# Seven products for the last pair of projections of the first unit, and three changes of order in the stages behind it

## Chip, cores and metric

The kernel runs on one core of a Trainium2 chip. The metric is the device time of one execution in microseconds (us), the median over several runs. The inputs and the outputs lie in the chip's memory; all of the arithmetic is float32, done on TensorE as pairs of fp32r parts (a rounded "hi" part and the remainder "lo").

## The reference

One layer of a streaming encoder, for 2048 frames of a new stream and 32 frames of a running one, width 1024:

```
hn   = rmsnorm(h, g_mix);  proj = hn @ w_in            # 1024 -> 3072
h_A, b_A, c_A, z_A, v_B, z_B = split(proj)             # six kinds of 512 columns
yA   = b_A * conv3(c_A * h_A) * silu(z_A)
yB   = (pooled(v_B) - v_B) @ pool_w * pool_scale * silu(z_B)
h    = h + concat(yA, yB) @ w_out
gate = sigmoid(rmsnorm(h, g_ple) @ w_ple_gate)
h    = h + (p @ w_ple) * gate                          # p: embedding frames, 256 wide
y    = rmsnorm(h, g_final)
```

The states of the convolution and of the pooling are returned too.

## The kernel before

**Stages.** (1) The input projection, from 0 to 532 us of the profile. (2) The first seven embedding products `p @ w_ple` (532 to 552 us). (3) The output projection with `w_out`, 16 tiles of 128 frames taken in pairs (552 to 717 us). (4) The other embedding products (717 to 747 us). (5) The gate with `w_ple_gate`, again in pairs of tiles, and the closing norm.

**Products.** A product of two fp32 operands is three matmuls per 128 rows of contraction: hi by hi, hi by lo, lo by hi (`FINE`). A weight or a frame is *put* into this form by a cast on ScalarE (hi) and a subtraction on VectorE (lo): `split`, L81 and L84, for frames and for the weights of stage 1, `weight_first` L203 and `weight_second` L210 for the weights of stages 3 and 5. In most places a two by two block product isn't done as eight half products but as seven (a Strassen-Winograd scheme): sums and differences of the blocks are put instead of the blocks, and three PSUM banks X, Y and Z gather the results. A half product is 12 matmuls of 128x512 (`half_product`, L646; in stages 3 and 5 `product`, L185).

**Stage 1.** The frames are taken in two groups of 1024 (two blocks of 512), and the 512 columns of each kind in four slices `j`. A `Unit` is one group and one slice. Its six kinds form the pairs zb and v, c and h, za and b. For all units but the first, `Unit.seven` runs the three pairs through `Unit.pair` (seven half products each; weights by `pair_weights`, whose sums and differences are L606 and L618 on VectorE). The first unit runs `Unit.plain`, since the normed, transposed frames and their sums are still being made: each kind is projected block by block (`project`, four half products for the two blocks, 48 matmuls), and a generator, `second_block`, makes the second block's frames and the differences T1 to T4 (L797) in twelve steps. `plain` calls `next(second)` where a step is to come in program order. T4 doesn't fit into the buffers at that time: its four quarters go to memory (`to_memory`, L546, the queue of GpSimd, POOL), and L1290 reads it back on SyncE's queue (SP) behind the unit, into a buffer (`seventh`) that the first unit's own frames (`B0_12`) hold until the last block-1 product has read them. The weights come through three raw buffers (`raw_weight`, L578) and six buffers of put weights (`wtile`).

**Who sets the order.** The program is written as a sequence of instructions, and the framework lists them for each engine before the run: by its own model of times it takes, among those that are ready, the one that stands first in the program. Each engine then runs its list strictly in order. `keep_in_program_order` (`pin`) ties an instruction behind the one written before it on its engine; `issue_after` ties the instructions of a block that are on one engine behind a given one. `bufs` of a pool says how many buffers of a tag there are; a new tile waits for the release of an old one.

**Stage 3, first pair of tiles (`o0`).** `seven(..., late=True)` runs X (frames A11 by weights 11), half of Z (S1 by T1), X (S2 by T2), the other half of Z, X (S3 by T3), then Y (A12 by 21), Z (S4 by 22) and X (A22 by T4). Carries of the banks X and Z are copies by ScalarE for this pair (L1320); the adds of the results are on VectorE (L1315). The functions in `LATER` are called between these products: `third` (weights T3), `left` (weights 21 and 22, then the frames' cast A12 by `more(0)`), `later(1)` (S4), `later("T4", 2)`. The differences for T2, T3 and T4 are L195; those of T3 are done by GpSimd before. The weight rows come in as `wo_t` (upper, `tops`) and `wo_b` (lower, `bots`).

**Stage 4.** L1501 loads the embedding's weights `wq` on SP, then the lower rows of the gate's weights (`wg_b`, L1386) are queued behind them with `issue_after(last_q.ins)`. The embedding frames `pps` (L129) come one tile of 128 frames after the other into the four buffers of the pool `st`, which the carries of stage 3 use too.

Of the kernel before, what the change touches and what calls it, by code (L numbers as in the profile page):

```python
# [36 lines left out]
def trunk(ctx, tc, x_p, x_s, c_conv, c_pool, p_p, p_s, g_mix, w_in, conv_w, conv_b, pool_w,  # L37
# [86 lines left out]
            wp.append(t)  # L124
        return wp

    def load_pps(t, i, queue):
        n = 4 * tiles[i][1]
        queue.dma_start(t.rearrange("p a k n -> p (a k n)")[:, :n].bitcast(F32), pp_d[i, :, :n])  # L129
        return t  # L130

    def short_embed_product(ps, pps, wp, cs, n):

# [51 lines left out]
                nc.tensor.matmul(ps[:n], lhs[:, k, a, :n], w[b][:, k], start=start and k + q == 0,  # L185
                                 stop=k == KH - 1 and q == 2, skip_group_check=True)

    def weight_source(W, q, k, top, bot, pin=False, sums=nc.vector):

        b11, b12 = top[:, :NH], top[:, NH:]  # L190
        b21, b22 = (bot[:, :NH], bot[:, NH:]) if bot is not None else (None, None)
        t, x, y = {"11": (b11, None, None), "T1": (b11, b12, b11), "T2": (b11, b22, b11), "T3": (b12, b22, b12),
                   "22": (b22, None, None), "21": (b21, None, None), "T4": (b21, b21, b11)}[q]
        if x is not None:
            ins = sums.tensor_tensor(t, x, y, op=ALU.subtract)  # L195
            if pin and sums is nc.vector:
                tc.keep_in_program_order(ins)
        return t

# [12 lines left out]
            tc.keep_in_program_order(ins)  # L212
        return ins

    def weight_parts(W, tops, bots, *names, order=range(KH), pin=False, sums=nc.vector):

        for q in names:
            at = lambda k: (W, q, k, tops[k], bots[k] if bots else None)
            todo = [(k, weight_source(*at(k), pin, sums)) for k in order[:2]]
            for k in order[2:]:  # L220
                weight_first(W, todo[0], q, pin)
                following = (k, weight_source(*at(k), pin, sums))
# [143 lines left out]
    def seventh(name):  # L366
        return w7.tile([P, 2 * KH * NH], F32R, tag="h", name=name)
# [31 lines left out]
    with ExitStack() as s1:  # L399
# [197 lines left out]
        def pair_weights(gi, ka, kb, j, name, ring, s_ring, ring_b, pin):  # L597

            s_t = (wk.tile([P, KH, P], F32, tag="s", name=f"s_{name}") if s_ring is None else
                   s_ring(f"s_{name}"))
            ra = raw_weight(ka, j, f"{name}a", ring)
            a11, a12 = ra[:, :KH], ra[:, KH:]
            sub = lambda o, x, y: nc.vector.tensor_tensor(o, x, y, op=ALU.subtract)  # L606
            if (ka, j) in kept:
                k1, k3 = kept.pop((ka, j))
                rb = ring_b(f"raw_{name}b")
                col = cols[kb] * WA + j * P  # L610
                nc.sync.dma_start(s_t, k1)
                nc.sync.dma_start(rb[:, :KH], k3)
                raw_loads.append(nc.sync.dma_start(rb[:, KH:], w_in[NH:, col:col + P].rearrange("(k p) n -> p k n", p=P)))
                s3, a22 = rb[:, :KH], rb[:, KH:]
            else:
                rb = raw_weight(kb, j, f"{name}b", ring_b)
                a21, a22 = rb[:, :KH], rb[:, KH:]
                total = nc.vector.tensor_tensor(s_t, a21, a22, op=ALU.add)  # L618
                if pin:
                    in_turn(total)  # L620
                sub(a21, a11, a21)
                s3 = a21
                if gi == 0:
# [212 lines left out]
        class Unit:  # L836
# [65 lines left out]
            def plain(self):  # L902
# [29 lines left out]
                for b in blocks:  # L932
                    ps = product_of("h", b, wh)
                    nc.vector.tensor_tensor(self.place(U, HU, b), ps, self.cols(c_s, b), op=ALU.mult)
                    self.conv(b)
                    if b:
                        next(second)
                wza = weights("za", j, f"za{tag}")
                for b in blocks:
                    z = self.cols(V, b)  # L940
                    nc.scalar.activation(z, product_of("za", b, wza), AF.Silu)
                    c = self.cols(c_s, b)
                    nc.vector.tensor_tensor(c, c, z, op=ALU.mult)
                    if b:
                        next(second)
                wb = weights("b", j, f"b{tag}")
                for b in blocks:
                    ps = product_of("b", b, wb)
                    y = self.cols(c_s, b)
                    nc.vector.tensor_tensor(y, ps, y, op=ALU.mult)  # L950
                    self.store(j, b, c_s)


            def pair(self, ka, kb, B, D, done, ring, s_ring=None, pin=False):
# [39 lines left out]
            def seven(self, B, aside, both=False):  # L994
# [24 lines left out]
                        self.conv(1)  # L1019


                za = [self.cols(V, b) for b in range(2)]
                gb = self.cols(U, 0)

                def za_done(b):
                    nc.scalar.activation(za[b], za[b], AF.Silu)
                    mul(self.cols(c_s, b), self.cols(c_s, b), za[b])

                def b_second():
                    mul(self.cols(c_s, 1), self.cols(c_s, 1), gb)  # L1030
                    self.store(j, 1, c_s)

                def b_first(ps):
                    mul(self.cols(c_s, 0), ps, self.cols(c_s, 0))
                    self.store(j, 0, c_s)

                ring = [spare_ring if both and i == 1 else raw_ring for i in range(3)]
                pairs = [
                    ("zb", "v", B, {(0, 0): self.cols(zs, 0), (0, 1): self.cols(zs, 1), (1, 1): at(V, HV, 1)},
                     {(0, 0): lambda ps: zb_done(0), (0, 1): lambda ps: zb_done(1), (1, 1): nothing, (1, 0): v_first}),  # L1040
                    ("c", "h", B, {(0, 0): self.cols(c_s, 0), (0, 1): self.cols(c_s, 1), (1, 1): at(U, HU, 1)},
                     {(0, 0): nothing, (0, 1): h_second, (1, 1): nothing, (1, 0): h_first}),
                    ("za", "b", B, {(0, 0): za[0], (0, 1): za[1], (1, 1): gb},
                     {(0, 0): lambda ps: za_done(0), (0, 1): lambda ps: (za_done(1), b_second()), (1, 1): nothing,
                      (1, 0): b_first})]

                def first_mix():
                    self.mix(0)
# [233 lines left out]
        for gi, tbs in enumerate(GROUPS):  # L1282
            if gi == 1:
                B = load_group(1)
            for j in range(4):
                u = Unit(gi, tbs, j)
                if gi + j == 0:
                    u.plain()
                    B0["T4"] = piece_of(seventh("B0_T4"), 0)
                    nc.sync.dma_start(B0["T4"].bitcast(F32), p_d["T4"])  # L1290
                    p_d["T4"] = tc.dram_tile([P, KH, 2, NB], F32, name="p_dT4b")
                    aside = at_pace(next_columns(3, 0, 1, 2), 13, 18)
                    continue
# [6 lines left out]
    with ExitStack() as s2:  # L1300
# [152 lines left out]
        gate_rows = iter(range(KC))  # L1453
        waiting = []

# [42 lines left out]
        got = {0: load_pps(st.tile([P, 2, 2, P], F32R, tag="t", name=f"pps_{EARLY}"), EARLY, nc.sync)}  # L1498
        for k in range(2):
            for h in range(2):  # L1500
                last_q = nc.sync.dma_start(wp[k][h].bitcast(F32), wl_d[k][h])  # L1501
# [327 lines left out]
```

## Time and profile before

| | |
|---|---|
| median of 3 runs | 930.83 us (930.36 to 932.89) |
| the profiled execution | 930.23 us |
| its span, first to last instruction | 928.4 us |
| TensorE (PE) busy | 902.4 us |
| VectorE (DVE) busy | 699.7 us |
| ScalarE (ACT) busy | 458.8 us |
| mean granted TensorE clock | 0.995 |

All starts below are us from the start of the span. A row of a timeline has the start, the duration, the engine, the line, the operation, out<-in, the count, and in brackets the idle time of the engine ahead of it with what ended it. Rows of several merged instructions have the duration from the first start to the last end. A row of a list of stretches has, for each engine, the busy time and the count, then the granted clock, the DMA engines' busy share and GB/s. A row of the DMA issues ends with the size and the us from issue to landing.

### The profile page before, as it was taken

What the parts mean: (1) busy time and instruction counts of PE and PEld (TensorE: products, weight loads), DVE (VectorE), ACT (ScalarE), POOL (GpSimd) and SP (SyncE); (2) the same over time, 40 slices, a digit from 0 to 9 for tenths busy, and PEclk for the clock granted to TensorE, in tenths of its full rate; (3) what the DMA queues carried; (4) which work ended last, traced back from release to release, by engine and by line L of the source; (5) the groups of instructions that cost most, each with busy time, mean ns of one, the idle gap of its engine ahead of it and who ended that gap; (6) DMA issues with size and microseconds to landing.
All of it is one profiled execution on the core that took longest, in us unless ns stands there. A gap on an engine that the chain in (4) does not pass through costs nothing. (4 is left out here: it accounts for less than half of the span.)

```text
span 928.4 us, 12196 instructions
## 1 busy us (share of the span) xinstructions
PE 902.4 (97%) x4186; PEld 724.1 (78%) x4186; DVE 699.7 (75%) x1144; ACT 458.8 (49%) x828; POOL 164.5 (18%) x313
## 2 busy tenths in 40 slices
PE   8999999999999999999999998999999899999996
PEld 6788887878788888766688876878888788778885
DVE  6895789797993688746668689765645988888884
ACT  7752555465453354523444366434434865555543
POOL 2200121222121123100010051111111211121212
PEclk9999999999999999999999999999999999999998
DMA  8164396747599776777743685886767776576653
GB/s 271 53 206 168 105 263 188 221 153 247 165 335 427 177 220 182 244 216 238 235 141 135 218 304 188 256 252 218 232 210 281 279 270 192 164 228 203 215 186 110
DMA packets 113243, 199.56 MB, mean 215 GB/s; under 512 B 13206, under 2 KB 69950, under 8 KB 112157
## 3 DMA queue, kind: packets, MB, share of 16 engines
q1 hardware_dynamic: 88733, 117.19, 40.5%
q0 software_dynamic: 22000, 77.21, 24.6%
q10 hardware_dynamic: 2448, 4.39, 1.3%
q8 instruction: 33, 0.54, 0.2%
q14 instruction: 29, 0.24, 0.1%
HBM read 133.06 MB, written 65.67 MB: 214 GB/s over the span
## 5 line engine op out<-in xcount | busy, mean ns | idle before, releaser
L185 PE MATMUL x_o<-wo_T,y_S 128*128 128x512 f32 x192 | 46.3, 390 | 1.3 <-ACT c_o L1320 1.3
L185 PE MATMUL z_o<-wo,y_S 128*128 128x512 f32 x192 | 47.6, 390 | 0.0
L185 PE MATMUL z_g<-wg,g_S 128*128 128x512 f32 x192 | 47.3, 392 | 0.0
L185 PE MATMUL x_o<-wo,y 128*128 128x512 f32 x192 | 45.5, 390 | 0.9 <-DVE x L1315 0.9
L185 PEld LDWEIGHTS x_o<-wo_T,y_S 128*128 128x128 f32 x192 | 35.9, 188 | 9.3 <-ACT c_o L1320 1.9
L185 PEld LDWEIGHTS x_o<-wo,y 128*128 128x128 f32 x192 | 36.0, 188 | 8.9 <-DVE x L1315 1.3
L185 PEld LDWEIGHTS z_o<-wo,y_S 128*128 128x128 f32 x192 | 36.0, 188 | 7.7 <-DVE y_S L84 0.3
L646 PE MATMUL z_ch<-B,w_ch_S 128*128 128x512 f32 x168 | 40.8, 392 | 1.1 <-ACT U L966 1.1
L646 PE MATMUL x_zab<-B,w_zab_S 128*128 128x512 f32 x168 | 41.1, 392 | 0.8 <-ACT V L966 0.6
L646 PE MATMUL x_ch<-B,w_ch_S 128*128 128x512 f32 x168 | 41.8, 392 | 0.0
L185 PEld LDWEIGHTS z_g<-wg,g_S 128*128 128x128 f32 x192 | 35.6, 188 | 7.4 <-ACT c_g L1553 0.2
L646 PE MATMUL z_zab<-B,w_zab_S 128*128 128x512 f32 x168 | 41.1, 392 | 0.0
L646 PE MATMUL x_zbv<-B,w_zbv_S 128*128 128x512 f32 x168 | 40.8, 391 | 0.0
L646 PE MATMUL z_zbv<-B,w_zbv_S 128*128 128x512 f32 x168 | 40.7, 391 | 0.0
L646 PEld LDWEIGHTS z_ch<-B,w_ch_S 128*128 128x128 f32 x168 | 31.3, 188 | 8.8 <-ACT U L966 1.5
L646 PEld LDWEIGHTS x_zab<-B,w_zab_S 128*128 128x128 f32 x168 | 31.2, 188 | 8.8 <-ACT V L966 1.0
L646 PEld LDWEIGHTS x_zbv<-B,w_zbv_S 128*128 128x128 f32 x168 | 31.3, 188 | 7.5 <-issue 0.8
L646 PEld LDWEIGHTS z_zab<-B,w_zab_S 128*128 128x128 f32 x168 | 31.2, 188 | 7.5 <-issue 0.8
L646 PEld LDWEIGHTS x_ch<-B,w_ch_S 128*128 128x128 f32 x168 | 31.3, 188 | 7.2 <-issue 0.8
L646 PEld LDWEIGHTS z_zbv<-B,w_zbv_S 128*128 128x128 f32 x168 | 31.3, 188 | 7.2 <-issue 0.8
L81 ACT CAST y_S<-y_fS 128x512 fp32r<-128x512 f32 x28 | 17.1, 619 | 26.5 <-PE x_o L185 12.1
L1572 DVE SCALAR_TENSOR_TENSOR h<-h,rstd_f,g_bc 128x1024 f32<-128x1024 f32 (+1 forms) x15 | 19.3, 1284 | 14.5 <-POOL rstd_f L77 12.9
(562 smaller groups left out, 2310.9 us busy)
## 6 DMA issues: line engine op xcount, KB each, us to landing
wn<-in_w_in_dram SPq DMA_DIRECT2D x24, 512.0 KB, 4.1
p_dT<-T POOLq DMA_DIRECT2D x16, 512.0 KB, 5.4
y<-y_d SPq DMA_DIRECT2D x16, 512.0 KB, 4.8
h<-h_d POOLq DMA_DIRECT2D x16, 512.0 KB, 4.8
e<-e_d SPq DMA_DIRECT2D x15, 512.0 KB, 4.6
x<-in_x_prompt_dram SPq DMA_DIRECT2D x14, 512.0 KB, 4.4
out_dram<-h POOLq DMA_DIRECT2D x14, 512.0 KB, 3.3
B<-p_d POOLq DMA_DIRECT2D x3, 2048.0 KB, 16.0
```

The costliest lines, as they stand in the source:

```text
L81: ins = nc.scalar.copy(hi, src)
L185: nc.tensor.matmul(ps[:n], lhs[:, k, a, :n], w[b][:, k], start=start and k + q == 0, stop=k == KH - 1 and q == 2, skip_group_check=True)
L646: nc.tensor.matmul(ps, lhs[:, k, x], b[:, k, y], start=start and k + q == 0, stop=stop and k == KH - 1 and q == 2, skip_group_check=True)
L1572: nc.vector.scalar_tensor_tensor(h[:n], h[:n], rf[:n], g_bc[:n], op0=ALU.mult, op1=ALU.mult)
```

## The change

Four edits:

1. The first unit's third pair (za, b) runs through `pair` with seven half products. `plain` calls `next(second)` in both rounds of `h` and no more behind them, T4 is read back ahead of the pair on POOL's queue, and the pair's dictionary moves into a method, `third`, that both `plain` and `seven` use. `pair_weights` doesn't keep the first unit's sums in memory.
2. In stage 4 the second embedding frames are loaded right behind `wq`, and the gate's lower rows are queued behind them.
3. T3's differences for `w_out` are done by VectorE, pinned.
4. In `LATER`, the cast of A12 comes ahead of the weights 21, and the weights 22 with S4 move to the next step.

```diff
-                if gi == 0:
+                if gi == 0 and j:
                     kept[ka, j] = k1, k3 = [tc.dram_tile(...)]
...
                     self.conv(b)
-                    if b:
-                        next(second)
-                wza = weights("za", j, f"za{tag}")
-                for b in blocks:
-                    z = self.cols(V, b)
-                    nc.scalar.activation(z, product_of("za", b, wza), AF.Silu)
-                    c = self.cols(c_s, b)
-                    nc.vector.tensor_tensor(c, c, z, op=ALU.mult)
-                    if b:
-                        next(second)
-                wb = weights("b", j, f"b{tag}")
-                for b in blocks:
-                    ps = product_of("b", b, wb)
-                    y = self.cols(c_s, b)
-                    nc.vector.tensor_tensor(y, ps, y, op=ALU.mult)
-                    self.store(j, b, c_s)
+                    next(second)
+                B0["T4"] = piece_of(seventh("B0_T4"), 0)
+                nc.gpsimd.dma_start(B0["T4"].bitcast(F32), p_d["T4"])
+                p_d["T4"] = tc.dram_tile([P, KH, 2, NB], F32, name="p_dT4b")
+                for _ in self.pair(*self.third(B0), raw_ring):
+                    pass
...
                 if gi + j == 0:
                     u.plain()
-                    B0["T4"] = piece_of(seventh("B0_T4"), 0)
-                    nc.sync.dma_start(B0["T4"].bitcast(F32), p_d["T4"])
-                    p_d["T4"] = tc.dram_tile([P, KH, 2, NB], F32, name="p_dT4b")
...
         def third():
-            hold.append(weight_parts(W, tops, bots, "T3", pin=True, sums=nc.gpsimd))
+            hold.append(weight_parts(W, tops, bots, "T3", pin=True))

         def left():
+            more(0)
             weight_parts(W, tops, bots, "21", pin=True)
+
+        def right():
             weight_slot(W, "wo", "22", "T4")
             hold.append(weight_parts(W, tops, bots, "22", pin=True))
-            more(0)
+            more(1)

-        LATER = {1: third, 2: left, 3: later(1), 4: later("T4", 2)}
+        LATER = {1: third, 2: left, 3: right, 4: later("T4", 2)}
...
         for k in range(2):
             for h in range(2):
-                last_q = nc.sync.dma_start(wp[k][h].bitcast(F32), wl_d[k][h])
-        with tc.issue_after(last_q.ins):
+                nc.sync.dma_start(wp[k][h].bitcast(F32), wl_d[k][h])
+        got[1] = st.tile([P, 2, 2, P], F32R, tag="t", name=f"pps_{EARLY + 1}")
+        second_pps = load_pps(got[1], EARLY + 1, nc.sync, True)
+        with tc.issue_after(second_pps.ins):
             bots = rows_of_weight(cmb, "wg_b", g_d, 1)[0]
```

More of the change, by code (lines that the diff above doesn't have):

```diff
@@ L125, in load_wp, with load_pps @@
         return wp
-    def load_pps(t, i, queue):
+    def load_pps(t, i, queue, ins=False):
         n = 4 * tiles[i][1]
-        queue.dma_start(t.rearrange("p a k n -> p (a k n)")[:, :n].bitcast(F32), pp_d[i, :, :n])
-        return t
+        load = queue.dma_start(t.rearrange("p a k n -> p (a k n)")[:, :n].bitcast(F32), pp_d[i, :, :n])
+        return load if ins else t
     def short_embed_product(ps, pps, wp, cs, n):
@@ L186, in product, with weight_source @@
                                  stop=k == KH - 1 and q == 2, skip_group_check=True)
-    def weight_source(W, q, k, top, bot, pin=False, sums=nc.vector):
+    def weight_source(W, q, k, top, bot, pin=False):
         b11, b12 = top[:, :NH], top[:, NH:]
@@ L194, in weight_source @@
         if x is not None:
-            ins = sums.tensor_tensor(t, x, y, op=ALU.subtract)
-            if pin and sums is nc.vector:
+            ins = nc.vector.tensor_tensor(t, x, y, op=ALU.subtract)
+            if pin:
                 tc.keep_in_program_order(ins)
@@ L213, in weight_second, with weight_parts @@
         return ins
-    def weight_parts(W, tops, bots, *names, order=range(KH), pin=False, sums=nc.vector):
+    def weight_parts(W, tops, bots, *names, order=range(KH), pin=False):
         for q in names:
             at = lambda k: (W, q, k, tops[k], bots[k] if bots else None)
-            todo = [(k, weight_source(*at(k), pin, sums)) for k in order[:2]]
+            todo = [(k, weight_source(*at(k), pin)) for k in order[:2]]
             for k in order[2:]:
                 weight_first(W, todo[0], q, pin)
-                following = (k, weight_source(*at(k), pin, sums))
+                following = (k, weight_source(*at(k), pin))
                 weight_second(W, todo.pop(0), q, pin)
@@ L935, in plain, with third, za_done, b_second @@
                     self.conv(b)
-                    if b:
-                        next(second)
-                wza = weights("za", j, f"za{tag}")
-                for b in blocks:
-                    z = self.cols(V, b)
-                    nc.scalar.activation(z, product_of("za", b, wza), AF.Silu)
-                    c = self.cols(c_s, b)
-                    nc.vector.tensor_tensor(c, c, z, op=ALU.mult)
-                    if b:
-                        next(second)
-                wb = weights("b", j, f"b{tag}")
-                for b in blocks:
-                    ps = product_of("b", b, wb)
-                    y = self.cols(c_s, b)
-                    nc.vector.tensor_tensor(y, ps, y, op=ALU.mult)
-                    self.store(j, b, c_s)
+                    next(second)
[4 more added lines that the diff above has]
+                    pass
+            def third(self, B):
+                j, V, c_s = self.j, self.V, self.c_s
+                mul = lambda o, x, y: nc.vector.tensor_tensor(o, x, y, op=ALU.mult)
+                za = [self.cols(V, b) for b in range(2)]
+                gb = self.cols(self.U, 0)
+                def za_done(b):
+                    nc.scalar.activation(za[b], za[b], AF.Silu)
+                    mul(self.cols(c_s, b), self.cols(c_s, b), za[b])
+                def b_second():
+                    mul(self.cols(c_s, 1), self.cols(c_s, 1), gb)
+                    self.store(j, 1, c_s)
+                def b_first(ps):
+                    mul(self.cols(c_s, 0), ps, self.cols(c_s, 0))
+                    self.store(j, 0, c_s)
+                return ("za", "b", B, {(0, 0): za[0], (0, 1): za[1], (1, 1): gb},
+                        {(0, 0): lambda ps: za_done(0), (0, 1): lambda ps: (za_done(1), b_second()), (1, 1): lambda ps: None,
+                         (1, 0): b_first})
             def pair(self, ka, kb, B, D, done, ring, s_ring=None, pin=False):
@@ L1019, in h_first @@
                         self.conv(1)
[L1022 to L1035, printed above, removed]
                 ring = [spare_ring if both and i == 1 else raw_ring for i in range(3)]
@@ L1042, in seven @@
                      {(0, 0): nothing, (0, 1): h_second, (1, 1): nothing, (1, 0): h_first}),
-                    ("za", "b", B, {(0, 0): za[0], (0, 1): za[1], (1, 1): gb},
-                     {(0, 0): lambda ps: za_done(0), (0, 1): lambda ps: (za_done(1), b_second()), (1, 1): nothing,
-                      (1, 0): b_first})]
+                    self.third(B)]
                 def first_mix():
```

## Prediction

> **What bounds the kernel now.** I read the page first (busy shares, then the slices with the granted clock), then TensorE's waits, then the timelines of TensorE, VectorE and ScalarE around each wait, and last the DMA issues with their times to landing.
>
> ```profile
> PE 902.4 (97%) x4186; PEld 724.1 (78%) x4186; DVE 699.7 (75%) x1144; ACT 458.8 (49%) x828; POOL 164.5 (18%) x313
> ...
> PE e L109 <- DMA pps<-pp_d: 3.2, 1, 3.2
> ...
> PE y_o L185 <- ACT y L81: 2.3, 1, 2.3
> ...
> PE x_o L185 <- ACT c_o L1320: 1.3, 1, 1.3
> ...
> PE x_o L185 <- DVE x L1315: 0.9, 1, 0.9
> ```
>
> TensorE is the bound: busy 902.4 of 928.4 us. Time goes only where matmuls go or a wait of TensorE goes. The four waits shown (us in total, times, longest) are where the edits aim: the first is the second embedding tile's, the others lie in the first pair of output tiles. A busy VectorE matters only where TensorE would wait for it.
>
> **Edit 1: the pair za, b.**
>
> ```profile
> 68.38 11.04 PE L646 MATMUL za<-B,w_za 128*128 128x512 f32 x48
> 79.26 11.04 PE L646 MATMUL b<-B,w_b 128*128 128x512 f32 x48
> 90.14 2.88 PE L646 MATMUL x_zbv<-B,w_zbv 128*128 128x512 f32 x12
> ```
>
> The 96 matmuls run from 68.38 to 90.14 with no gap, 0.2267 us each. Seven half products are 84. **Removed: 12 x 0.2267 = 2.72 us.** Added on VectorE: 4 sums or differences, 3 more lo parts, 3 adds of results, 10 operations; on ScalarE 3 casts and 3 carries. Between two such VectorE operations lie 0.60 us (next fence, 68.30 to 68.90), so 6.0 us, ScalarE about 3.6.
>
> ```profile
> 59.75 1.29 DVE L84 TENSOR_TENSOR w_za<-raw_za,w_za 128x512 fp32r<-128x512 f32 x2
> ...
> 68.30 0.69 DVE L84 TENSOR_TENSOR w_b<-raw_b,w_b 128x512 fp32r<-128x512 f32 x1
> 68.90 0.68 DVE L934 TENSOR_TENSOR U<-h,c_s 128x512 f32<-128x512 f32 x1
> ...
> 71.44 0.68 DVE L84 TENSOR_TENSOR T<-f,T 128x512 fp32r<-128x512 f32 x1
> ...
> 68.00:72.00 4.00, 4.00 (x19) 3.31 (x18) 4.00 (x8) 1.95 (x3) 0.00 (x0) 1.00 0.16 65
> ...
> 78.00:80.00 2.00, 2.00 (x11) 1.65 (x10) 0.09 (x1) 0.54 (x2) 0.00 (x0) 1.00 0.00 0
> ```
>
> VectorE is full up to 72 us (4.00 of 4 us) and pauses at 78 (0.09 of 2), so the 6 us are hidden as a sum, but not the first of them. The za weights' two lo parts at 59.75 stand in the program ahead of the fourth quarter of the second block's frames; the pair's weights stand behind it. So the fourth quarter moves up by those 1.2 us and by the w_b parts among it, and its last operation (T, 71.44) comes at about 69. The pair's sum S1, difference S3 and first lo part find gaps only from about 67.7 on, among U (68.90) and the convolution: three operations and these end at 70.8. TensorE could start at 68.38, has two matmuls of X and two of Y that need no lo part (0.9 us), and waits until 70.8: 1.5. The wait that takes the removed matmuls' place is this one. Bounds: 0, if the sums find gaps before, and 3.0 (a lo part at the old place of T, 71.44). I take 2.0: between them, nearer the upper row since VectorE shows no gap. The later weights need at most two operations in each 2.72 us.
>
> T4 now is needed in the pair:
>
> ```profile
> 72.41 0.85 POOL L546 DMA_DIRECT2D p_dT<-T  x1 [9.63 <-DVE T L84]
> ...
> p_dT<-T POOLq DMA_DIRECT2D x1, 512.0 KB, 4.3
> ...
> B_T<-p_dT SPq DMA_DIRECT2D x1, 2048.0 KB, 8.7
> ...
> B<-p_d POOLq DMA_DIRECT2D x2, 2048.0 KB, 13.9
> ```
>
> Its last quarter goes out at 72.41, or 70 if T comes at 69, and lands 4.3 later; then POOL reads 2048 KB, in 8.7 us as SP did alone, or 13.9 as POOL did among other loads. So it lands at 70 + 4.3 + 8.7 = 83.0 at best, at 72.4 + 4.3 + 13.9 = 90.6 at worst. The seventh product is due at 68.38 + 72 x 0.2267 + 2.0 = 86.7. The DMA engines idle at 78 to 80 (0.00), so I take the lone row: hidden, cost 0; bound 4.0. The buffer is free in time, as the last reader is h's second block, over before 68. Behind the waiting POOL instruction nothing is due before 90. Sum: -2.72 + 2.0 = **-0.7 us**, from -2.7 to +4.3.
>
> **Edits 3 and 4: the first pair of output tiles.**
>
> ```profile
> 544.92 4.21 DVE L84 TENSOR_TENSOR y_S<-y,y_S 128x512 fp32r<-128x512 f32 x2 [0.23 <-ACT y_S L81]
> ...
> 552.56 1.92 DVE L210 TENSOR_TENSOR wo_T<-wo_t,wo_T 128x512 fp32r<-128x512 f32 x1
> ...
> L195 POOL TENSOR_TENSOR wo_t<-wo_b,wo_t x4: 1298/1304/1702, 545.3 to 552.6; 128x512 f32<-128x512 f32 x4
> L195 DVE TENSOR_TENSOR wo_t<-wo_b,wo_t x4: 676/678/1778, 549.7 to 554.4; 128x512 f32<-128x512 f32 x4
> ```
>
> While GpSimd makes a T3 difference (1.30 us), VectorE's operation beside it takes 1.8 to 2.2 us instead of 0.68: two at 544.92 together 4.21, one of L195 1.78, one at 552.56 1.92. That is 4.21 + 1.78 + 1.92 - 4 x 0.68 = 5.2 us lost; the edit gives them back and puts 4 x 0.60 = 2.4 on VectorE. T2 then is ready some 4 us sooner, except its last row, which lands late (next fence: 543.64 + 6.6 = 550.2), so T2 ends at about 552.7.
>
> ```profile
> 543.64 0.55 POOL L1410 DMA_DIRECT2D wo_b<-in_w_out_dram  x1 [6.22 <-DMA y_d<-c_s]
> ...
> wo_b<-in_w_out_dram POOLq DMA_DIRECT2D x1, 512.0 KB, 6.6
> ...
> 554.46 1.52 PE L185 MATMUL z_o<-wo,y_S 128*128 128x512 f32 x6
> ...
> 556.59 0.60 ACT L1320 COPY c_o<-x_o 128x512 f32<-128x512 f32 x1
> ...
> 563.32 0.62 ACT L81 CAST y<-y 128x512 fp32r<-128x512 f32 x1
> ...
> 563.84 0.59 ACT L1320 COPY c_o<-x_o 128x512 f32<-128x512 f32 x1
> ...
> 573.07 0.67 DVE L1315 TENSOR_TENSOR x<-x_o,x 128x512 f32<-128x512 f32 x1
> ...
> 573.79 1.45 PE L185 MATMUL x_o<-wo,y 128*128 128x512 f32 x5 [0.85 <-DVE x L1315]
> ```
>
> With T2 early, the first carry (556.59) can go at 554.5, and the 1.3 us wait ends. With weights 22 pinned behind the second carry, the cast at 563.32 and the carry at 563.84 come before four casts of 0.5, and most of the 2.3 us wait ends. But VectorE is late next: TensorE's X by T4 at 573.79 waits for the add at 573.07, the end of a full run of VectorE. From the first carry's end (555.1) and T3's first cast (0.6) on, it has to do 4 lo parts and a difference of T3, 4 of 21, 1 of A12, 4 of 22, 1 of S4, 8 of T4, 1 of A22 and 3 adds: 27 x 0.60 = 16.3, so 572.1 against 573.74. **-1.65 us.** The waits before become one before X by T4. Bounds: -4.45 (all three waits) and 0.
>
> **Edit 2: the second embedding tile.**
>
> ```profile
> 709.09 1.76 SPq L1501 DMA_DIRECT2D wq<-wl_d  x4
> ...
> 710.90 1.89 SPq L1386 DMA_DIRECT2D wg_b<-g_d  x4
> ...
> 712.58 0.68 DVE L1315 TENSOR_TENSOR x<-x_o,c_o 128x512 f32<-128x512 f32 x1
> ...
> 714.99 0.68 DVE L1315 TENSOR_TENSOR x<-y_o,c_o 128x512 f32<-128x512 f32 x1
> ...
> 713.29 23.81 SPq L129 DMA_DIRECT2D pps<-pp_d  x8
> ...
> pps<-pp_d SPq DMA_DIRECT2D x1, 256.0 KB, 10.7
> ...
> pps<-pp_d SPq DMA_DIRECT2D x1, 256.0 KB, 9.9
> ...
> 724.03 20.88 PE L109 MATMUL e<-wq,pps 128*128 128x512 f32 x84 [3.21 <-DMA pps<-pp_d]
> ...
> 744.74 2.01 PE L137 MATMUL e<-wq,pps 128*64 128x512 f32 x8
> ...
> 724.00:725.00 1.00, 0.97 (x2) 0.83 (x3) 1.00 (x3) 1.00 (x3) 0.00 (x0) 0.50 1.01 410
> ```
>
> The second tile's issue at 713.29 waits for a buffer of `st`, which the add at 712.58 frees, not for the queue; it then lands 10.7 us later, at 724.0, behind 2 MB of `wg_b`. TensorE idles 3.21 us and starts at half its clock (0.50 at 724): 84 matmuls take 744.74 - 724.03 = 20.71 where 84 x 0.2267 = 19.04 would do, 1.67 more. The wait costs 4.9 us in all. After the edit the second tile goes at 713.29 and lands by about 718, behind `wq` alone; TensorE starts at 720.8 and is through at 723.5. `wg_b` follows at 713.7 instead of 710.9. The third tile's load, issued when the add at 714.99 frees the next buffer (715.7), then is behind the same bytes as the second was, plus 256 KB: 724.0 + 0.6 = 724.6 at 410 GB/s, or 715.7 + 9.9 = 725.6 as now. I take 724.9: a new wait of 1.4, too short for the clock. Then 72 x 0.2267 = 16.3, end 741.2 against 744.74: **-3.5 us**, from -4.9 (no wait) to 0 (given back behind it, where the gate's first products need frames and weights that a full VectorE makes).
>
> **Sum.** -0.7 - 1.65 - 3.5 = -5.85 on the profiled execution, which took 930.23 (span 928.4): 924.4. The median of the runs shown is 0.6 higher, so 925.0.
>
> **The rivals.** (a) All of it comes: 2.72 + 4.45 + 4.9 = 12.1, so 918.8. For: each wait has one named releaser; against: VectorE's full run at 68 to 72, and its place as the releaser at 573.79.
>
> (b) POOL's read takes 13.9, as among other loads: a wait of 2 to 4.0 before the seventh product, 927 to 929.
>
> (c) Given back: the waits of the first pair of output tiles, now one before X by T4, reach the 3.2 us after which the clock halved at 724, and 1.67 more makes edits 3 and 4 worth nothing; and edit 2 is lost to the gate's frames: 930.8 - 0.7 = 930. For: VectorE is the releaser there already (573.79). [...]
>
> (d) Slower: T4's round trip through memory. If the 10 added operations push T from 71.44 to 77.4, it goes out at 77.7, is there at 82.0, is read by 95.9; TensorE waits 9.2 us from 86.7, and 1.67 for the clock: 925.0 + 10.9 = 936. It decides from a last store at about 75 on. Against it: T stands ahead of the pair in the program.
>
> [...]
>
> **How the numbers follow.** Forecast 0.44, (a) 0.12, (b) 0.15, (c) 0.14, (d) 0.10, (e) 0.05. A measurement of this kernel tells 0.3%, 2.8 us, from no change. Faster: forecast, (a), two thirds of (b): 0.66. Same: a third of (b), (c), (e): 0.24. Slower: (d), 0.10. The range takes in the forecast with its bounds, the nearer half of (a), (b) and (c): 919.5 to 930.5; (d), (e) and the far end of (a) are left out, 0.2.
>
> **What would show it.** Edit 1: 84 matmuls from about 68.4, a wait of 1 to 2 us in the first product, none before the one that reads T4. Edits 3 and 4: no VectorE operation of 2 us at 545 to 553; the waits for ScalarE gone, one for L1315 left. Edit 2: no wait before the second embedding tile, one of about 1.4 before the third, the clock at 1.00. It is wrong if TensorE waits for `B_T`, or if the gate's first pair gets waits that it hasn't now.

## The result and the profile after

The changed kernel takes 940.4 us (median of 4 runs, 936.64 to 942.71) against 931.09 (4 runs, 930.36 to 932.89). The ratio is 1.009 (95% interval 1.0068 to 1.0112): it is 0.9% slower, where 925.0 was forecast. The profiled execution took 942.71 us, with a span of 940.9; it is the slowest of the four, 2.3 us over their median. First the waits of TensorE in the changed kernel (us in total, times, longest):

```profile
PE pth L1525 <- ACT ho L1523: 5.3, 2, 4.7
PE pt L484 <- ACT xt L794: 4.3, 1, 4.3
PE x_o L185 <- DVE x L1308: 3.9, 2, 3.4
...
PE e L109 <- DMA pps<-pp_d: 1.3, 1, 1.3
```

Of the four waits that the edits aimed at, two are gone and the second embedding tile's has become one of 1.3 us. The fourth, ahead of X by T4 in the first output pair, has grown from 0.9 to 3.4 us. Two more, the first two lines, stand at places where the kernel before had none. The timeline of TensorE, before and after, says how much each cost. Before, those starts that the prediction doesn't show:

```profile
57.50 11.04 PE L646 MATMUL h<-B,w_h 128*128 128x512 f32 x48
...
551.74 2.88 PE L185 MATMUL x_o<-wo,y 128*128 128x512 f32 x12
...
578.95 1.67 PE L185 MATMUL z_o<-wo,y_S 128*128 128x512 f32 x6
...
746.59 2.90 PE L185 MATMUL x_g<-wg,g 128*128 128x512 f32 x12
...
755.57 2.98 PE L185 MATMUL z_g<-wg,g_S 128*128 128x512 f32 x12
```

After:

```profile
36.95 1.11 PE L484 MATMUL pt<-ident,xt 128*128 128x128 f32 x4 [4.34 <-ACT xt L794]
37.71 3.76 PE L680 MATMUL v<-B,w_firstv 128*128 128x512 f32 x8
...
64.71 11.04 PE L646 MATMUL h<-B,w_h 128*128 128x512 f32 x48
75.59 2.88 PE L646 MATMUL x_zab<-B,w_zab 128*128 128x512 f32 x12
...
94.63 2.88 PE L646 MATMUL x_zbv<-B,w_zbv 128*128 128x512 f32 x12
...
557.45 2.88 PE L185 MATMUL x_o<-wo,y 128*128 128x512 f32 x12
...
578.08 6.85 PE L185 MATMUL x_o<-wo,y 128*128 128x512 f32 x22 [3.43 <-DVE x L1308]
584.77 1.52 PE L185 MATMUL z_o<-wo,y_S 128*128 128x512 f32 x6
...
732.65 16.60 PE L109 MATMUL e<-wq,pps 128*128 128x512 f32 x72 [1.34 <-DMA pps<-pp_d]
...
750.94 2.90 PE L185 MATMUL x_g<-wg,g 128*128 128x512 f32 x12
...
764.04 1.97 PE L1525 MATMUL pth<-ident,ho 128*128 128x128 f32 x8 [4.74 <-ACT ho L1523]
765.66 4.73 PE L185 MATMUL z_g<-wg,g_S 128*128 128x512 f32 x12
```

Read as differences of the starts:

| to the start of | before | after | later by | this stretch |
|---|---|---|---|---|
| h of the first unit | 57.50 | 64.71 | 7.2 | +7.2 |
| the next unit (x_zbv) | 90.14 | 94.63 | 4.5 | -2.7 |
| the first output pair (x_o) | 551.74 | 557.45 | 5.7 | +1.2 |
| the second output pair's z_o | 578.95 | 584.77 | 5.8 | +0.1 |
| the gate (x_g) | 746.59 | 750.94 | 4.35 | -1.5 |
| the gate's first z_g | 755.57 | 765.66 | 10.1 | +5.7 |
| the end of the span | 928.4 | 940.9 | 12.5 | +2.4 |

Edit 1's 2.7 and edit 2's gain are both there (the fifth row is -3.4 at the embedding and +2.0 in the rest of stage 3). Two stretches lose 12.9 us: the start, ahead of all products of the pair, and the gate's first pair. In both, the matmuls that follow an idle stretch also run slowly: 8 matmuls of v in 3.76 us for 2.08, the 12 of z_g in 4.73 for 2.98 (which falls in the last row).

The start, in the timelines of SyncE, VectorE and ScalarE after:

```profile
31.13 0.37 SPq L578 DMA_DIRECT2D raw_zab_0b<-in_w_in_dram  x1
...
30.38 0.69 DVE L765 TENSOR_TENSOR w_firstc<-raw_firstc,w_firstc 128x512 fp32r<-128x512 f32 x1
34.98 0.69 DVE L618 TENSOR_TENSOR s_zab<-raw_zab_0b 128x512 f32<-128x512 f32 x1 [3.92 <-DMA raw_zab_0b<-in_w_in_dram]
35.59 1.28 DVE L84 TENSOR_TENSOR B<-pt,B 128x512 fp32r<-128x512 f32 x2
...
36.31 1.18 ACT L794 COPY xt<-pt 128x512 f32<-128x512 f32 x2 [5.29 <-DVE B L84]
```

and before, VectorE and the same load:

```profile
30.54 1.28 DVE L84 TENSOR_TENSOR B<-pt,B 128x512 fp32r<-128x512 f32 x2
...
30.68 0.37 SPq L578 DMA_DIRECT2D raw_b<-in_w_in_dram  x1
```

The same load of b's weights goes out at the same place of both kernels, when the first weights' last lo part (30.38 after) has read its buffer. Before, nobody wants it for a long time (ScalarE's first cast of it is at 54.30). After, the pair's sum S1 (L618) stands right behind that lo part in VectorE's list, more than 40 us before TensorE needs anything of it, and VectorE waits in order: 3.92 us for the load. The frames' lo parts (L84, 35.59) stand behind it, ScalarE's copy out of the same PSUM bank behind those, and TensorE's next transposes (36.95) behind that.

### The profile page after: what moved, and what is told of

Its sections match the earlier page's. It is cut to its first block, busy times and chain, and to the rows that moved or that the text cites. A ratio compares the mean times of both kernels' runs of the same rounds, so it can differ in the third digit from the quotient of the medians.

```text
span 940.9 us, 12187 instructions
## 1 busy us (share of the span) xinstructions
PE 906.1 (96%) x4174; PEld 726.2 (77%) x4174; DVE 702.5 (75%) x1158; ACT 460.2 (49%) x834; POOL 161.4 (17%) x310
## 4 chain that ended last, share of the span: by engine, by line
PE 49%; DMA 13%; DVE 7%; issue 7%; ACT 2%; POOL 1%; POOLq 0%; ACTq 0%; DVEq 0%; SPq 0%
PE x_g L185 8%; PE x_o L185 5%; PE z_g L185 4%; PE x_ch L646 4%; PE e L109 4%; PE x_zab L646 4%; DMA raw_zab_0b<-in_w_in_dram 4%; PE x_zbv L646 3%; PE z_ch L646 2%; DMA gs<-in_w_ple_gate_dram 2%; PE z_o L185 2%; PE z_zab L646 2%; PE y_g L185 2%; DMA hn<-h_d 2%; DMA B<-p_d 2%
## 5 line engine op out<-in xcount | busy, mean ns | idle before, releaser
L646 PE MATMUL x_zab<-B,w_zab_S 128*128 128x512 f32 x192 | 46.8, 392 | 0.6 <-ACT V L979 0.4
L646 PE MATMUL z_zab<-B,w_zab_S 128*128 128x512 f32 x192 | 46.8, 392 | 0.0
L646 PEld LDWEIGHTS x_zab<-B,w_zab_S 128*128 128x128 f32 x192 | 35.7, 188 | 9.5 <-issue 0.8
L646 PEld LDWEIGHTS z_zab<-B,w_zab_S 128*128 128x128 f32 x192 | 35.7, 188 | 8.5 <-issue 0.8
L646 PEld LDWEIGHTS z_ch<-B,w_ch_S 128*128 128x128 f32 x168 | 31.3, 188 | 8.9 <-ACT U L979 1.7
L646 PEld LDWEIGHTS x_zbv<-B,w_zbv_S 128*128 128x128 f32 x168 | 31.3, 188 | 8.4 <-ACT zs L979 1.2
L646 PEld LDWEIGHTS x_ch<-B,w_ch_S 128*128 128x128 f32 x168 | 31.3, 188 | 7.2 <-issue 0.8
L646 PEld LDWEIGHTS z_zbv<-B,w_zbv_S 128*128 128x128 f32 x168 | 31.3, 188 | 7.2 <-issue 0.8
L84 DVE TENSOR_TENSOR y_S<-y_fS,y_S 128x512 fp32r<-128x512 f32 x28 | 19.1, 688 | 16.4 <-ACT y_S L81 16.4
```

Source lines behind the costliest of these rows:

```text
L84: eng.tensor_tensor(lo, src, hi.bitcast(F32), op=ALU.subtract)
L646: nc.tensor.matmul(ps, lhs[:, k, x], b[:, k, y], start=start and k + q == 0, stop=stop and k == KH - 1 and q == 2, skip_group_check=True)
```

## The experiments

All kernels were timed beside the kernel before. Each ratio is to it, with its 95% interval.

**Edit 1 by itself, `edit1_alone`.** The diff is the first edit's part of the change.

> The kernel before with edit 1 alone. Theory: nearly all that was lost comes from here. VectorE's list has the pair's sum S1 (L618) right behind the first weights' lo parts, and there it waits for b's raw weights (3.92 us in the changed kernel); what ScalarE and TensorE then lack costs 7.2 us by the start of h, clock included; the pair gives 2.7 back, and stage 1 adds about 1. So the time is 4.5 to 6 us over the kernel before, 935.5 to 937. Rival: the late start belongs to that execution (its first frames also landed 0.56 us later) or to the other edits; then edit 1 gives its 2.7 us, and the time is 928 to 929.

Measured: 937.77 us, ratio 1.0078 (1.0066 to 1.009). In its profile the wait ahead of the transposes is 4.28 us, and the next unit starts at 93.55, 3.4 later than before. The median is 0.8 us above the expected range. So edit 1 makes up 6.6 of the 9.3 us that the change lost, and the late start isn't a matter of one execution.

**The sums held back, `sums_last`.** Edit 1, and in `pair_weights`:

```diff
-                if pin:
+                if pin or gi + j == 0:
                     in_turn(total)
-                sub(a21, a11, a21)
+                s3_ins = sub(a21, a11, a21)
+                if gi + j == 0:
+                    in_turn(s3_ins)
```

> Edit 1 alone, with the pair's sum S1 and difference S3 tied in program order behind the last step of the second block's frames, so that VectorE's list can't have them early. Theory: the 3.92 us of idle VectorE at 31 us and the 4.3 us of TensorE go, h starts at about 57.5 as before, and the pair's first product waits 1.5 to 2 us for its lo part, as the prediction had it: 930 to 931, 0 to 1 us below the kernel before. Rival: the start is late because the second block's frames now have a step in the first round of h, or because VectorE has more to do; then h stays late and the time at 935 or more.

Measured: 931.12 us, ratio 1.0006 (0.9993 to 1.0019). TensorE's and VectorE's timeline:

```profile
31.32 1.28 DVE L84 TENSOR_TENSOR B<-pt,B 128x512 fp32r<-128x512 f32 x2
...
69.19 2.88 PE L648 MATMUL x_zab<-B,w_zab 128*128 128x512 f32 x12
...
76.25 2.60 PE L648 MATMUL x_zab<-B,w_zab_S 128*128 128x512 f32 x10 [0.24 <-DVE w_zab_S L84]
...
89.11 2.88 PE L648 MATMUL x_zbv<-B,w_zbv 128*128 128x512 f32 x12
...
724.78 21.36 PE L109 MATMUL e<-wq,pps 128*128 128x512 f32 x84 [4.51 <-DMA pps<-pp_d]
```

The order of two operations of VectorE is worth 6.6 us: nothing else differs from `edit1_alone`. The pair now takes 89.11 - 69.19 = 19.92 us against 21.76 before, 1.84 less. The expected wait of 1.5 to 2 us in the first product doesn't come; 0.24 does, two products on, and with short gaps beside it the pair is 0.9 us over the 19.04 of its 84 matmuls. But the kernel as a whole isn't faster: here the second embedding tile is waited for 4.51 us (3.21 before). That tile landed at 724.78, 0.75 us later than before, although TensorE was 0.55 us earlier at the stage's first product: what was gained ahead of the landing was waited for there.

**The sums a little earlier, `sums_after_conv`.** As above, and the pair's generator is made and advanced once behind `self.conv(0)`.

> As sums_last, but S1 and S3 stand in program order behind the convolution of h's first block, ahead of the second block's last frames. Theory: the sums are done before TensorE is through with h, no wait ahead of the pair, and edit 1 gives its whole 2.7 us: 928 to 929. Rival: VectorE is full there, so the two operations only push the last frames and T4 back by 1.2 us, and TensorE waits for those instead: 929.5 to 931, no better than sums_last.

Measured: 932.34 us, ratio 1.0019 (1.0005 to 1.0033). Two matmuls of X and two of Y, then a wait of 1.31 us for the first lo part (`w_zab`, L84); the pair takes 20.64 us. The rival was right that earlier sums are no better than late ones, but not in its reason: TensorE waited for the first lo part, not for the second block's last frames or for T4, and the time is above both expected ranges. In the profiled execution the gate's transposes, too, waited 2.50 us, and this without edit 2.

**Edits 3 and 4, `edits34_alone`, and each by itself, `edit3_alone` and `edit4_alone`.** The diffs are those of the change.

> The kernel before with edits 3 and 4 alone. Theory: the two waits for ScalarE in the first pair of output tiles go and come back as one wait of about 3.4 us for VectorE's add ahead of X by T4, long enough for a slow clock behind it (22 matmuls in 6.85 us for 5.3): -1.4 and +1.5, so 931, within 0.5 of the kernel before. Rival (the prediction's term): the merged wait stays short, and 1.65 us remain: 929.5.

> The kernel before with edit 3 alone (T3's differences by VectorE). Theory: the waits of the first pair of output tiles are merged by edit 4's order, not by this; here VectorE's three slow stretches beside GpSimd go and its own four differences come, the wait for the first carry (1.26 us) goes, the one for A12's cast (2.34) stays, and the add ahead of X by T4 comes some 0.5 us sooner or later: 930.5 to 931.5. Rival: VectorE's four operations more make it late, and this edit is what makes the 3.4 us wait: 932 or more.

> The kernel before with edit 4 alone (A12's cast ahead of the weights 21, the weights 22 a step later; T3's differences stay with GpSimd). Theory: the 2.34 us wait ends and comes back ahead of X by T4, where VectorE is late; together with the 0.85 there it reaches 3 us and the slow clock: 931.5 to 932.5. Rival: VectorE has slack enough without edit 3, the wait stays at about 2, and 929.5 to 930.5 come out.

Measured: both 932.68, ratio 1.0015 (1.0 to 1.003); edit 3 930.81, 0.9998 (0.9984 to 1.0012); edit 4 933.2, 1.0014 (1.0002 to 1.0026). The first output pair with both:

```profile
552.23 2.88 PE L185 MATMUL x_o<-wo,y 128*128 128x512 f32 x12
...
573.02 6.86 PE L185 MATMUL x_o<-wo,y 128*128 128x512 f32 x22 [3.42 <-DVE x L1315]
...
572.20 0.67 DVE L1315 TENSOR_TENSOR x<-x_o,x 128x512 f32<-128x512 f32 x1
```

From X's first product to X by T4 it is 20.79 us for 22.05 before, so 1.26 are gained; the slow clock then takes 6.86 - 5.32 = 1.54. With edit 4 alone the wait is 3.04 us and the clock slow as well (22 matmuls in 6.87 us). With edit 3 alone there are two waits, 2.02 and 1.42 us, with 36 matmuls between them; the clock stays, and the profiled execution is 1.45 us ahead behind the pair. So the joined wait is edit 4's. By the medians the two can't be told apart so surely, as their intervals overlap a little.

In their profiles, the joined wait isn't all that the two kernels with edit 4 lost, and the rest is at a place that neither edit touches. At the gate's first product `edits34_alone` is 1.0 us ahead of the kernel before (745.58 to 746.59) and `edit4_alone` level with it (746.62); by the end of the span they are 2.0 and 3.4 us behind. The gate's first transposes wait 1.28 and 1.86 us there, and a product behind them another 0.7 us in each. The part on edit 2 below comes back to this wait.

**The wait parted again, `edits34_add_first`.** Edits 3 and 4, and:

```diff
-        LATER = {1: third, 2: left, 3: right, 4: later("T4", 2)}
+        LATER = {1: third, 2: left, 3: right, 5: later("T4", 2)}
```

> Edits 3 and 4, with T4's weights and A22 one step later in the program (step 5 for 4), so that VectorE takes the add that frees the bank X as soon as X by S3 and T3 is through, ahead of T4's lo parts. Theory: edits 3 and 4 lose by the one long wait and its slow clock; with the add out of the way only T4's own weights are late, the wait is under 2.5 us and the clock stays: 929 to 930. Rival: T4's weights are as late as the add was, since VectorE is full and has the same work: the wait stays at 3 us or more, 931.5 to 932.5.

Measured: 932.2 us, ratio 0.9999 (0.9985 to 1.0012).

```profile
573.43 2.56 PE L185 MATMUL x_o<-wo,y 128*128 128x512 f32 x10 [2.28 <-DVE y L84]
577.37 2.58 PE L185 MATMUL x_o<-wo,y 128*128 128x512 f32 x10 [1.38 <-DVE y L84]
...
724.51 20.96 PE L109 MATMUL e<-wq,pps 128*128 128x512 f32 x84 [2.38 <-DMA pps<-pp_d]
```

Place and mechanism are as expected: two waits of 2.28 and 1.38 us, 10 matmuls in 2.56 us, so the full clock. Idle time was not saved, 3.66 us in all. From X's first product to the next pair's Z this execution takes 26.49 us (553.30 to 579.79), 1.0 less than `edits34_alone` (27.49) and 0.7 less than before (27.21). But 2.28 us is close to what was followed by half clock elsewhere: behind a wait of 2.33 us in `sums_after_conv` 12 matmuls took 4.15 us for 2.9. By the ratios the time is 0.16% below `edits34_alone`, but the intervals overlap, and the expected 929 to 930 didn't come.

**Edit 2, `edit2_alone`, and with the mended pair, `fix1_edit2`.**

> The kernel before with edit 2 alone. Theory: the embedding products end 3.4 us sooner, but VectorE's work for the gate's weights starts when the lower rows land and stays full, the buffers that the next frames need come free no sooner, and the gate's first pair waits 4 to 5 us ahead of its transposes, with a slow clock behind: 5 to 6 us given back, so 932 to 934. Rival: the gate's wait in the changed kernel comes from the other edits (stage 3's last sums later); then the 3.4 us stay: 927.5 to 928.

> The kernel before with edit 1, its sums tied behind the second block's frames (as in sums_last), and edit 2. Theory: the pair gives 1.8 us, which the second embedding tile's wait took back in sums_last (4.51 us for 3.21); with edit 2 this wait is gone, so both gains arrive at the gate, 4 to 5 us, and there the transposes of the next frames, whose load goes out when VectorE frees its buffers, take back 0 to 7 of it: 928 to 931, with executions spread by several us. Rival: the gate's transposes always wait as long as in the changed kernel (4.7 us and the clock): 932 or more.

Measured: 931.72 us (11 runs, 928.51 to 935.18), ratio 1.0006 (0.9994 to 1.0019), and 931.79 us (12 runs, 928.84 to 935.84), ratio 1.001 (0.9994 to 1.0026). In the profiled execution of `edit2_alone`, 929.04 us, the gate's transposes didn't wait at all: the next frames arrived just in time, and 1.2 us of span were left. So the theory's constant loss of 5 to 6 us is wrong; the loss depends on when the next frames land. The rival's 927.5 to 928 didn't come either: that execution is one of the fastest of the 11, their median shows no gain, and where the slower ones lost it was not seen. `fix1_edit2` is 0.8 us above the expected 928 to 931, with the expected spread. In its profile the wait is there:

```profile
741.46 2.49 DVE L1768 TENSOR_TENSOR wg_b<-wg_b,wg_t 128x512 f32<-128x512 f32 x4
...
744.91 0.64 SPq L396 DMA_DIRECT2D hn<-h_d  x1
...
754.30 1.14 ACT L1522 COPY ho<-hn 128x512 f32<-128x512 f32 x2 [6.06 <-DMA hn<-h_d]
...
754.98 1.97 PE L1524 MATMUL pth<-ident,ho 128*128 128x128 f32 x8 [3.66 <-ACT ho L1522]
```

VectorE's four differences for T4 (L1768) are the last readers of the upper gate rows, whose buffers the next frames (`hn`) take: SyncE's loads go out as the differences are done, the last one at 744.91. It lands some 9 us later, and only then can ScalarE copy it and TensorE transpose it.

**The differences moved ahead, `fix1_edit2_diffs`, and the transposes moved back, `fix1_edit2_both`.** The first:

```diff
-        weight_parts(W, tops, bots, "21", "22")
+        weight_parts(W, tops, bots, "21")
         for k in range(KH):
             nc.vector.tensor_tensor(bots[k][:, :NH], bots[k][:, :NH], tops[k][:, :NH], op=ALU.subtract)
+        weight_parts(W, tops, bots, "22")
```

The second has also:

```diff
-            return {2: first, 3: second}
+            return {3: first, 4: second} if ahead else {2: first, 3: second}
```

> As fix1_edit2, with T4's four differences for the gate, whose end frees the buffers of the next frames' loads, ahead of the weights 22 in the program: 4 operations of 0.6 us earlier. Theory: the loads go out 2.4 us sooner, the wait ahead of the transposes gets 2.4 us shorter and too short for the slow clock: 2 to 4 us below fix1_edit2, at 925 to 928. Rival: the loads' landing is set by the other transfers at that time (POOL's of h, the stores of the embedding), not by their issue: then nothing changes against fix1_edit2.

> As fix1_edit2_diffs, with the next frames' transposes of the gate's first pair one product later (the steps 3 and 4 for 2 and 3). Theory: another 2.7 us of cover for the loads, so no wait is left there: 925 to 926, and a smaller spread. Rival: the frames made from the transposes are then late for the next pair, or VectorE holds the later products: 927 or more.

Measured: 930.21 us (928.65 to 931.92), ratio 0.9987 (0.9973 to 1.0001), and 930.5 us (926.69 to 932.75), ratio 0.9985 (0.9968 to 1.0001). In neither profile do the gate's first transposes wait. `fix1_edit2_diffs`:

```profile
743.72 0.42 SPq L396 DMA_DIRECT2D hn<-h_d  x1
...
744.21 2.90 PE L185 MATMUL x_g<-wg,g 128*128 128x512 f32 x12
...
752.84 1.04 PE L1524 MATMUL pth<-ident,ho 128*128 128x128 f32 x8
```

The last load goes out 0.5 us ahead of the gate's first product; in `fix1_edit2` it was 2.0 us behind it (744.91 to 742.94). Of these 2.5 us, 1.2 are the load's, and 1.3 come from an embedding stage that happened to end later. The wait of 3.66 us is gone, the slowest run is 931.92 instead of 935.84, and the median is 1.6 us lower, though the two intervals just overlap. The expected 925 to 928, and 925 to 926 with a smaller spread for `fix1_edit2_both`, didn't come: this profile and that of `fix1_edit2_both` lose ahead of the gate instead, the latter by a wait of 2.81 us at the third embedding tile and 72 matmuls in 19.44 us behind it (16.60 at full clock).

**All of it, `all_mended`.** All four edits with the changes of `sums_last`, `fix1_edit2_diffs` and `edits34_add_first`.

> All four edits with the three mends: the pair's sums tied behind the second block's frames, T4's differences of the gate ahead of the weights 22, and T4's weights of the first output pair one step later. Theory: the single terms add up: -1.8 from the pair, -1 to -1.5 from the first output pair, -3.4 at the embedding and no wait at the gate, less what the transfers at 700 to 730 us take back (1 to 3): 925 to 928.5, below both kernels. Rival: what is gained ahead of the embedding stage is only waited out there, as its transfers set its end; then 929 to 930.5, as without edits 3 and 4.

Measured: 929.34 us (12 runs, 926.62 to 934.4), ratio 0.9976 (0.9959 to 0.9993). It is faster than the kernel before by 0.24%, and by the two ratios than the changed one by about 1.1%. Its waits at the places in question:

```profile
571.22 2.59 PE L185 MATMUL x_o<-wo,y 128*128 128x512 f32 x10 [2.26 <-DVE y L84]
...
575.19 2.58 PE L185 MATMUL x_o<-wo,y 128*128 128x512 f32 x10 [1.38 <-DVE y L84]
...
725.50 16.60 PE L109 MATMUL e<-wq,pps 128*128 128x512 f32 x72 [1.66 <-DMA pps<-pp_d]
```

The clock stays at both, and the gate's first transposes have no wait. The four edits are thus worth something, some 2 us, once each of the three orders that they broke is mended. The single terms (1.8, 1 to 1.5 and 3.4) still don't add up in the end, and the expected 925 to 928.5 was missed by 0.8 us.

## Why the prediction was wrong, step by step

**What bounds it.** Right: TensorE, and only waits and matmuls moved the end. Busy time went from 902.4 to 906.1 us with 12 matmuls fewer; the rise is slow clock.

**Edit 1, the failed step.** The prediction priced the pair's operations on VectorE where they are *needed* (S1, S3 and the first lo part "find gaps only from about 67.7 on") and looked for a wait at TensorE. An earlier place stood in it only as a gain ("0, if the sums find gaps before"). It didn't ask where the list could place them *earliest*. S1 needs nothing but a raw weight, and so was placed at 31 us, behind nothing but a load. That the list's model of times took this load to be there follows from the place; the profile doesn't show the model. The wait wasn't in any term or rival: "slower" stood for T4's round trip alone. The price: 7.2 us up to h (4.34 of idle TensorE, some 2.7 of slow clock behind it, less 0.3 by two later waits; 0.45 were there already at 15.95, from the first frames' landing; it is 6.1 in `edit1_alone`), and 6.6 us of the median between `edit1_alone` and `sums_last`. Step by step otherwise: -2.72 for the matmuls held (75.59 to 94.63 is 19.04); the wait of 2.0 for the first lo part was 0 in the changed kernel, since the sums were long done, and with the sums held back 0.24 (0.9 with the gaps beside it). In `sums_after_conv` it came as the prediction describes it: two matmuls of X, two of Y, then a wait of 1.31 until 70.79, where 1.5 until 70.8 was worked out. So what failed is the place of the sums in the list, not the price of the pair. T4's read was hidden, as forecast: neither (b) nor (d) came, and no run shows a term for (e).

```profile
82.29 0.57 POOL L938 DMA_DIRECT2D B_T<-p_dT  x1 [3.70 <-DMA p_dT<-T]
...
91.91 2.88 PE L646 MATMUL x_zab<-B_T,w_zab 128*128 128x512 f32 x12
```

The read went out 9.6 us ahead of its product and landed 8.3 us later, so no wait came, nor did one in the seven other profiles with edit 1: the lone row's 8.7 us was the right one, not the 13.9. (The forecast has h's second block over before 68; it ended at 68.5, which changes nothing.)

**Edits 3 and 4.** VectorE's chain was sized well: 20.36 us from X's first product to the end of the add were forecast (572.1 - 551.74), and 572.87 - 552.23 = 20.64 measured. The gain of 1.65 was 1.26 (1.42 in the changed kernel). A second, smaller step failed here: the wait that is left had no term for the clock in the sum. What the forecast left to rival (c) came: the joined wait, 3.42 us, halves the clock, and that costs 1.54. (c) had chance 0.14, though its condition followed from the forecast's own numbers: three waits of 1.26, 2.34 and 0.85 become one, and taking 1.65 off their 4.45 leaves 2.8, near the 3.21 of the row at 724.03. The waits of 3.04 and 3.42 us before the 22 matmuls were both followed by the slow clock (6.87 and 6.86 us for 5.32), as the 3.21 of that row was.

**Edit 2.** Right in place and size in the changed kernel: -3.4 at the embedding for -3.5, with a wait of 1.34 before the third tile for 1.4 (2.25 in `edit2_alone`). The forecast said what would take it back, "frames and weights that a full VectorE makes", and left it out of the sum; its bound for the edit was 0, all of the gain given back. It came, at the next frames' loads, in a size that changes from run to run: 0 in one profile of `edit2_alone`, 3.66 us in `fix1_edit2`, 4.74 in the changed kernel, where the last copy came this late:

```profile
749.44 2.49 DVE L1769 TENSOR_TENSOR wg_b<-wg_b,wg_t 128x512 f32<-128x512 f32 x4
...
763.37 1.14 ACT L1523 COPY ho<-hn 128x512 f32<-128x512 f32 x2 [7.15 <-DMA hn<-h_d]
```

There the differences ended 1.0 us behind the gate's first product (750.94); before, they had ended 2.5 us ahead of it. So the last load went out 1.7 us behind that product and not 0.8 ahead of it, and it also took longer: 10.7 us (752.63 to 763.37) for 5.9 (745.82 to 751.69). With the slow clock behind the wait this is more than edit 2 gained, so the bound of 0 was wrong in this execution. Why the load was slower wasn't followed.

A stage that is made shorter takes the cover from what the next one loads during it. The profiles without edit 2 bear this out. From the embedding stage's first product to the gate's first product it is 29.5 us in the kernel before, and 28.8 to 31.3 in the four others where the gate's first transposes didn't wait. Where the stage happened to be shorter, they did: 26.5 us in `edits34_alone`, 27.2 in `sums_after_conv` and 27.5 in `edit4_alone`, with waits of 1.28, 2.50 and 1.86 us.

**The sum.** The single medians add up: edit 1 +6.6, edit 2 +0.6, edits 3 and 4 +1.6 make +8.8, and the whole change is +9.3; edit 2's +0.6 is within its interval. The +1.2 us in the rest of stage 1 and the +2.0 in the rest of stage 3 are small waits at several places and weren't followed.

## What to carry to other kernels

An operation that needs only a load can be put, by whoever orders the program, wherever its inputs are thought to be there; on an engine that runs its list in order it then holds up all that is behind it (here VectorE, for 3.92 us). So price each new operation at its earliest place as well as at its due one, and tie it where it is due. When waits of TensorE are joined or a stage gets shorter, ask two more things: whether the one wait that is left is long enough to slow the clock (3.04 and 3.42 us were, here), and which loads of the next stage were hidden behind the time that is gone.

## What the runs showed of the hardware

How long TensorE idled before its clock halved wasn't one number here. In `edits34_add_first` an idle stretch of 2.38 us was enough (stretch, length, TensorE's busy time and matmuls, granted clock, DMA share, GB/s):

```profile
724.00:725.00 1.00, 0.49 (x2) 1.00 1.04 401
725.00:726.00 1.00, 1.00 (x5) 0.60 1.03 422
...
728.00:729.00 1.00, 1.00 (x5) 0.69 0.64 254
```

A mean of 0.60 over 725 to 726 is half clock from 725.2 on, 0.7 us after TensorE is at work again; the 0.69 says that it lasts until 728.6, 3.4 us later. In `edit4_alone` a stretch of 2.75 us at the same place left the clock at 1.00, and 84 matmuls took 19.34 us instead of 20.96:

```profile
725.59 19.34 PE L109 MATMUL e<-wq,pps 128*128 128x512 f32 x84 [2.75 <-DMA pps<-pp_d]
```

In the changed kernel the clock falls three times before TensorE's last matmul:

```profile
35.00:36.00 1.00, 0.00 (x0) 0.76 0.00 0
...
578.00:579.00 1.00, 0.92 (x3) 0.62 1.09 353
...
762.00:763.00 1.00, 0.00 (x0) 0.78 1.03 414
```

Read in the same way, it falls at 35.52, 578.24 and 762.56 us, for 6.84, 3.42 and 6.84 us. The idle stretches there are 4.34, 3.43 and 4.74 us long, and at the first and the third fall TensorE is still idle (0.00 in the rows at 35 and 762).

In all 14 profiles, between 25 and 900 us of the span, TensorE idled 16 times for 2.25 to 2.75 us. By the pace of the matmuls behind them, half clock followed seven of these stretches, of 2.33 to 2.53 us. It followed each of the eleven stretches of 2.81 to 4.74 us, and none of those of 1.2 to 2.02 us. What decides among the 16 was not shown.

For a sum it means that, in these kernels, stretches between 2.25 and 2.75 us cost about 1.6 us (84 matmuls in 20.96 us for 19.34) or nothing; all of 2.81 us or more were followed by half clock. The wait of 2.34 us in the kernel before, for A12's cast, shows the luck: it stands unchanged in eight of the profiles, with 2.33 to 2.36 us, and the clock fell behind it in four of them. The waits of 2.28 and 2.26 us in `edits34_add_first` and `all_mended` left the clock alone: 10 matmuls took 2.56 and 2.59 us.
